# A two-layer encoder trunk in split float32: priority of one pair's sums, a scheduling edge for pair 0's accumulating transfers, and earlier low parts for the first mixer's output weights

## The chip, the cores and the metric

One NeuronCore of a Trainium2 chip runs the whole program. The metric is the device time of one execution in microseconds; of several runs the median counts. The engines are named as in the profile: PE is TensorE, DVE is VectorE, ACT is ScalarE, POOL is GpSimd, and SP is SyncE, which here only issues transfers.

## The reference

Two request groups, 512 and 256 tokens of 1024 numbers, go through the same trunk with the same weights. Nothing mixes the groups, so the kernel lays them side by side as 768 columns.

```
def even_layer(x, ...):
    x = x + 0.5 * swiglu(rmsnorm(x, f1_n), f1_g, f1_u, f1_d)
    x = x + mixer_ab(rmsnorm(x, mix_n), w_in, ..., w_out)
    x = x + 0.5 * swiglu(rmsnorm(x, f2_n), f2_g, f2_u, f2_d)
    return x

def odd_layer(x, ...):      # the same with mixer_c in the middle
    ...

def mixer_ab(h, w_in, ..., sink, w_out):
    z = h @ w_in
    a_out = u * vmix        # chunked spatial gating, u and v out of gelu(z[:, :1024])
    b_out = window_gqa(rope_partial(q), rope_partial(k), v, sink)
    return concatenate([a_out, b_out], axis=-1) @ w_out
```

The hidden width of the SwiGLU is 2816. A final rmsnorm follows the two layers.

## The kernel before

**Split float32.** Every product is made of three matmul passes on two-part numbers. A float32 tile is split into a high part, which is a rounded copy (`whi`, `oh`, `th`), and a low part, the difference (`wlo`, `ol`, `tl`). `wsplit` (L112) does it for weights: ACT makes the high part at L122, and DVE or POOL, by its argument `eng`, the low part at L123. POOL is the default. `split` (L206) does it for activations, always with ACT at L208 and DVE at L209. `mm3` (L188) then issues three matmuls of up to 512 columns at L152: high weight by high operand, high weight by low operand, low weight by high operand.

**The blocks.** Four half SwiGLU blocks (`ffn`) and two mixers alternate. In a block the gate and up weights are worked through in 11 pairs of 128-column tiles, by a scheme with seven products for a two-by-two blocking. It needs sums of weight tiles (`sums`, named `s1` to `s4`, L737). In the first four pairs (`EARLY`) the two products that need only the first half of the tokens come first, over all four pairs in the sequence `ORDERS`; each product's result is copied from PSUM by ACT into a tile `p1` (L602), and those copies are noted in the list `copied`. The first sum `s1` of these pairs isn't made by DVE but by the transfers: `added` loads one weight tile into a tile `s` and then a second one on top of it with an accumulating transfer. Both are issued by POOL at L107. For pair 0 this is called once, in the loop at the end of `ffn`, behind the ninth step of the sequence.

**The first mixer's end.** `mixer0` computes spatial gating and windowed attention; eight tiles `o` of 128 rows collect their outputs. `mixer_out` (L970) multiplies them by the output weights and adds the result to the residual, which was kept in DRAM (`xdm`) and comes back into tiles `xold`. Column tiles are called m = 0 to 7. `rows(m)` prepares the weights of one column tile: for even m it loads a 512 KB tile and a 256 KB tile `raw` by SP and splits the small one (for this and the next m, low part on DVE), then it splits its own half of the large one (low part on POOL). The tiles m = 0 and 1 (`alone`) are prepared ahead and begun while the attention of the last blocks still runs: k-tiles 4 and 5 first, then 0 to 3, first for the first 384 columns, then for the rest. After that the loop over m = 2 to 5 prepares and multiplies one column tile after the other. The attention chain is interleaved with it: scores on PE, mask and maximum on DVE (L1099), exponentials on ACT (L1105), scaling on DVE (L1115), transposes on PE (L156), `th` and `tl`, values on PE, and their sum into `o` on DVE (L1250).

**What sets the order.** PE's order is that of the code, with the interleaved chains placed by a counter of estimated PE time. On the other engines a list scheduler picks at compile time among ready instructions, by their place in the code and by `high_priority`; each engine then runs its list strictly in that order. `issue_after(ins)` queues those instructions of its block that run on the engine of `ins` behind `ins` in that list. It is no wait at run time. Tiles come from rotating pools: four `raw` buffers, five `whi` and five `wlo`. A transfer into a reused buffer waits until the last reader is done, and behind it waits all that SP has still to issue.

Of the kernel before, what the change touches and what calls it, by code (L numbers as in the profile page):

```python
# [16 lines left out]
P = 128  # L17
# [27 lines left out]
EARLY = 4  # L45
# [10 lines left out]
class Trunk:  # L56
# [421 lines left out]
    def ffn(self, pre):  # L478
# [2 lines left out]
            self.fw = self.open("work", self.other(self.guards["comb"][1]))  # L481
        rt, scales = self.acc, self.scales
        mixed = bool(self.unfed)
        urgent = 0 if self.first else EARLY - 1
        hs = {}

        etile = self.etile
# [36 lines left out]
        entries, entered, addeds = {}, {}, {}  # L524

        def pair(p):
# [12 lines left out]
            h = hs[p] = {}  # L539
# [3 lines left out]
            def sums(n, name):  # L543
                return self.sums(a[n, 1, 1], a[n, 1, 2], a[n, 2, 1], a[n, 2, 2], s, n, name)

            def parts(n, b):
                name = {"t2": "s2", "t3": "s3", "t1": "s1", "b22": "s4"}.get(b)
                with self.tc.high_priority() if b == "t2" and p == urgent else nullcontext():
                    return self.wsplit(sums(n, name) if name else a[n, 2, 2], nc.vector)

            def product(n, w, b, key, start, st=None):
# [95 lines left out]
            def entry():  # L647
                load((0, 1))
                return parts("gate", "t2")

            def settle(st):

                todo = [(n, b) for b in ("t2", "t3", "n4", "t1", "b22") for n in names]
                key = {"t1": "Z", "b22": "Z"}
                for i, (n, b) in enumerate(todo):
                    now, st = st, None
                    if i + 1 < len(todo):
                        st = parts(*todo[i + 1])
                    elif p + 1 < EARLY and (p % 2 or not p):
                        entered[p + 1] = entries[p + 1]()  # L660
                    if b == "t2":
                        begin(n, e[n, "p1"])
                    product(n, None, b, key.get(b, "Y"), b == "t1", now)
                    if b in ("t2", "t3"):
                        keep(b.replace("t", "u"), "Y", n)
                    elif b == "n4":
                        next(steps, None)
                    else:
                        add("Z", n, "u3" if b == "t1" else "u2")
                    if n == "up":  # L670
                        if b == "n4":
                            hidden(1, 0, bank["Y", "gate"], bank["Y", "up"])
                        elif b == "t1":
                            hidden(1, 1, e["gate", "u3"], e["up", "u3"])
                        elif b == "b22":
                            hidden(0, 1, e["gate", "u2"], e["up", "u2"])
# [30 lines left out]
        for i, p in enumerate(ORDERS[mixed]):  # L707
            next(stages[p])
            if i == 8:
                addeds[0]()  # L710
        for p in range(NPAIR):
            for _ in stages[p]:
                pass
# [256 lines left out]
    def mixer_out(self, name, ot, chain, cols=False, begun=None):  # L970

        nc = self.nc
        early, late = (4, 5, 0, 1, 2, 3) if cols else range(KD - 2), (KD - 2, KD - 1)
        oh, ol = ([self.gp.tile([P, T], F32R, tag=f"x{n}{k}", name=f"o{n}{k}") for k in range(KD)] for n in "hl")
        src = (oh, ol)
        self.x = [None] * KD
        old = {}

        def parts(ks, h):
            c0, c1 = HALVES[h]
            for k in ks:
                self.split(oh[k][:, c0:c1], ol[k][:, c0:c1], ot[k][:, c0:c1])

        def ready(ks, done=()):
            for h in (0, 1):
                parts([k for k in ks if (k, h) not in done], h)
            for k in ks:
                self.x[k] = self.xp.tile([P, T], F32, tag=f"x{k}", name=f"x{k}")  # L990
                if not cols:
                    nc.sync.dma_start(self.x[k], self.xd[k])

        def put(m, h, ps):

            c0, c1 = HALVES[h]
            x = self.x[m]
            if not cols:
                nc.vector.tensor_tensor(out=x[:, c0:c1], in0=ps[:, :H], in1=x[:, c0:c1], op=ALU.add)
                return  # L1000
            if h == 0:
                old[m] = self.rawp.tile([P, T], F32, tag="raw", name="xold")
                nc.sync.dma_start(old[m], self.xd[m])
            for a, b in ((H, TA), (TA, T)) if h else ((0, H),):
                out, rows = self.by_column(x, slice(0, P), a, b)
                nc.vector.tensor_tensor(out=out, in0=rows(ps[:, a - c0 : b - c0]), in1=rows(old[m][:, a:b]), op=ALU.add)

        def plus(m, h, ps):
            x = self.x[m][:, HALVES[h][0] : HALVES[h][1]]
            nc.vector.tensor_tensor(out=x, in0=ps[:, :H], in1=x, op=ALU.add)  # L1010
            self.final(m, *HALVES[h])

        loaded = {}

        def rows(m):
            if m % 2 == 0:
                loaded[4] = self.raw(name, 0, 4, m * P, 2 * P)
                loaded[2] = self.unit(name, 4, 2, m * P, 2 * P)
            c = m % 2 * P
            hi, lo = self.wsplit(loaded[4][:, :, c : c + P])  # L1020
            return [(hi[:, k, :], lo[:, k, :]) for k in range(4)] + [tuple(t[:, c : c + P] for t in k) for k in loaded[2]]

        def first(m, h, w):
            put(m, h, self.proj(w, src, HALVES[h], ks=early))

        def second(m, h):
            st = [tuple(t[:, k, m % 2 * P : m % 2 * P + P] for t in ends[m // 2]) for k in (0, 1)]
            plus(m, h, self.proj([None] * 6 + st, src, HALVES[h], ks=late))

        def end(i):  # L1030
            if i % 2 == 0:
                loaded["end"] = self.raw(name, KD - 2, 2, i * 2 * P, 4 * P)
            c = i % 2 * 2 * P
            ends.append(self.wsplit(loaded["end"][:, :, c : c + 2 * P]))

        alone = ()
        if begun:
            alone = (0, 1)
            w = [rows(m) for m in alone]
            done = [self.proj(w[m], begun, (0, H), ks=early[:2], last=False) for m in alone]  # L1040
            rest = early[2:]
            with self.tc.high_priority(), self.tc.issue_after(self.exps[-1]):
                parts(rest, 0)
            for m in alone:
                ps = self.proj(w[m], src, HALVES[0], ps=done[m], ks=rest, first=False)
                if m == 0:
                    parts(early, 1)
                    parts(early[:2], 0)
                    ready(early, [(k, h) for k in early for h in (0, 1)])
                put(m, 0, ps)  # L1050
            for m in alone:
                first(m, 1, w[m])
        else:
            ready(early)
        for m in range(len(alone), KD - 2):
            w = rows(m)
            for h in (0, 1):
                first(m, h, w)
        self.drain(chain)
        with self.tc.issue_after(self.exps[-1]):  # L1060
            self.silu()
        ready(late)
        self.ffn_open(self.close("mp"))
        self.ffn_tiles()
        self.mixed = True
        self.norm_begin(self.following)
        ends = []
        w = rows(6)
        end(0)
        first(6, 0, w)  # L1070
        end(1)
        for m in (0, 1):
            second(m, 0)
        first(6, 1, w)
        for m in (2, 3):
            second(m, 0)
        w = rows(7)
        end(2)
        for h in (0, 1):
            first(7, h, w)  # L1080
        end(3)
        for m in range(4, KD):
            second(m, 0)
        self.half_done(0)
        for m in range(KD):
            second(m, 1)
        self.close("xg")
        self.fw = self.open("work", self.other(self.guards["comb"][1]))
        self.half_done(1)
# [732 lines left out]
```

## Time and profile before

| | us |
|---|---|
| three runs, median (lowest to highest) | 2595.53 (2593.48 to 2601.28) |
| the profiled execution | 2594.83 |
| its span | 2593.1 |
| PE busy | 2552.5 |
| DVE busy | 2231.6 |
| ACT busy | 1366.2 |
| POOL busy | 159.3 |

The span runs from the first to the last instruction; the execution's own time is 1.7 us longer. PE's granted clock was 0.997 of full speed over the span. Rows of the timeline give start, duration, engine, line, operation and tiles; in brackets stands the idle time ahead of the row and what ended it. An instruction's duration overlaps the next one's start a little, so the distance from start to start is what one costs in a full queue.

### The profile page before, as it was taken

How to read it: one execution, taken by the hardware profiler on the slowest of the kernel's cores; microseconds unless marked ns; L12 is line 12 of the kernel's file. 1: busy time of each engine (PE TensorE's matmuls, PEld its weight loads, DVE VectorE, ACT ScalarE, POOL GpSimd, SP SyncE). 2: the span in 40 equal slices, each digit the busy share in tenths (PEclk: the TensorE clock that was granted, in tenths of full speed). 3: DMA queues.
4: the chain of work that ended last, by engine and by line, in shares of the span. 5: the costliest groups of instructions: out<-in, count | busy, mean ns of one | idle time of the engine just before them, and what ended most of it. 6: DMA issues, size and time to landing. Idle time of an engine off the chain costs nothing.

```text
span 2593.1 us, 41320 instructions
## 1 busy us (share of the span) xinstructions
PE 2552.5 (98%) x15114; PEld 2487.0 (96%) x15114; DVE 2231.6 (86%) x4659; ACT 1366.2 (53%) x2869; POOL 159.3 (6%) x255
## 2 busy tenths in 40 slices
PE   9999999999999999999999999999999999999998
PEld 8999999988899999999999999998998999999997
DVE  7988898889789989889998889986767699888897
ACT  7544454556656545445654445454545465444543
POOL 1000000000121000000100000001222220000000
PEclk9999999999999999999999999999999999999999
DMA  7523222421144322222532222242221343222212
GB/s 256 160 85 102 72 80 68 134 90 52 50 128 130 114 66 74 74 72 92 142 103 82 66 82 66 66 145 64 64 64 41 106 134 119 82 72 76 72 65 75
DMA packets 93372, 238.68 MB, mean 92 GB/s; under 512 B 21488, under 2 KB 34288, under 8 KB 93168
## 3 DMA queue, kind: packets, MB, share of 16 engines
q1 hardware_dynamic: 85712, 218.96, 26.4%
q0 software_dynamic: 7168, 16.78, 3.0%
q8 instruction: 119, 1.95, 0.3%
q14 instruction: 85, 0.70, 0.1%
q10 hardware_dynamic: 288, 0.29, 0.0%
HBM read 226.56 MB, written 15.07 MB: 93 GB/s over the span
## 4 chain that ended last, share of the span: by engine, by line
PE 67%; DVE 4%; ACT 1%; issue 1%; DMA 0%; DVEq 0%; ACTq 0%
PE ps_mm L152 41%; PE ps_aux L152 25%; PE ps_aux L156 1%; DMA raw<-in_w 0%; DVE wlo L123 0%; DVE tmp L415 0%; ACT p L1105 0%; DVE p L1115 0%; DVE p L1099 0%; ACT whi L122 0%; DVE s L737 0%; DVE tl L209 0%; DVE qk L1579 0%; DVE sg L589 0%; DVE t21l L209 0%
## 5 line engine op out<-in xcount | busy, mean ns | idle before, releaser
L122 ACT CAST whi<-s 128x512 fp32r<-128x512 f32 x496 | 304.7, 620 | 408.2 <-DVE s L737 184.3
L122 ACT CAST whi<-raw 128x512 fp32r<-128x512 f32 x504 | 305.9, 619 | 226.6 <-PE ps_mm L152 93.5
L123 DVE TENSOR_TENSOR wlo<-s,whi 128x512 fp32r<-128x512 f32 x496 | 336.7, 684 | 60.2 <-ACT whi L122 52.6
L123 DVE TENSOR_TENSOR wlo<-raw,whi 128x512 fp32r<-128x512 f32 x468 | 320.1, 692 | 18.6 <-ACT whi L122 15.0
L152 PE MATMUL ps_aux<-dt,whi 128*128 128x384 f32 x864 | 219.2, 334 | 0.0
L152 PE MATMUL ps_mm<-db,whi 128*128 128x384 f32 x864 | 219.2, 334 | 0.0
L152 PEld LDWEIGHTS ps_aux<-dt,whi 128*128 128x128 f32 x864 | 156.0, 188 | 0.0
L152 PEld LDWEIGHTS ps_mm<-db,whi 128*128 128x128 f32 x864 | 156.0, 188 | 0.0
L152 PE MATMUL ps_aux<-dt,wlo 128*128 128x384 f32 x432 | 144.4, 334 | 1.4 <-DVE wlo L123 1.4
L152 PE MATMUL ps_mm<-xh,whi 128*128 128x512 f32 (+1 forms) x416 | 145.6, 350 | 0.0
L152 PE MATMUL ps_mm<-db,wlo 128*128 128x384 f32 x432 | 144.3, 334 | 0.0
L152 PE MATMUL ps_mm<-xh,wlo 128*128 128x512 f32 (+1 forms) x416 | 140.9, 339 | 0.0
L152 PE MATMUL ps_mm<-xl,whi 128*128 128x512 f32 (+1 forms) x416 | 140.9, 339 | 0.0
L737 DVE TENSOR_TENSOR s<-raw,raw 128x512 f32<-128x512 f32 x124 | 84.0, 685 | 26.6 <-DMA raw<-in_w 26.3
L577 DVE TENSOR_TENSOR u<-ps_aux,u 128x384 f32<-128x384 f32 x176 | 96.9, 551 | 4.6 <-PE ps_aux L152 4.3
L152 PE MATMUL ps_aux<-dh,whi 128*128 128x384 f32 x384 | 97.5, 334 | 0.0
L793 DVE TENSOR_TENSOR x<-ps_aux,x 128x384 f32<-128x384 f32 x160 | 85.2, 550 | 14.1 <-PE ps_aux L152 13.9
L1105 ACT ACTIVATE p<-p,st 128x256 f32<-128x256 f32 (+3 forms) x144 | 68.9, 480 | 50.2 <-DVE st L1103 50.1
L123 POOL TENSOR_TENSOR wlo<-raw,whi 128x512 fp32r<-128x512 f32 x36 | 48.5, 1355 | 720.8 <-ACT whi L122 707.3
L572 ACT COPY u<-ps_mm 128x384 f32<-128x384 f32 x176 | 83.5, 474 | 17.0 <-PE ps_mm L152 16.6
L793 DVE TENSOR_TENSOR x<-ps_mm,x 128x384 f32<-128x384 f32 x160 | 86.0, 550 | 6.9 <-PE ps_mm L152 6.6
L107 POOL DMA_DIRECT2D s<-in_w x64 | 47.0, 762 | 700.6 <-PE ps_aux L152 387.0
(516 smaller groups left out, 8172.7 us busy)
## 6 DMA issues: line engine op xcount, KB each, us to landing
raw<-in_w SPq DMA_DIRECT2D x346, 512.0 KB, 3.7
s<-in_w POOLq DMA_DIRECT2D x64, 256.0 KB, 5.0
xdm<-x SPq DMA_DIRECT2D x16, 384.0 KB, 2.4
x<-in_x SPq DMA_DIRECT2D x16, 192.0 KB, 5.9
tok<-in_xt SPq DMA_DIRECT2D x12, 256.0 KB, 6.7
xold<-xdm SPq DMA_DIRECT2D x8, 384.0 KB, 3.1
x<-xdm SPq DMA_DIRECT2D x8, 384.0 KB, 4.7
out_y<-y SPq DMA_DIRECT2D x8, 384.0 KB, 2.4
```

Source lines behind the costliest of these rows:

```text
L107: (eng or self.nc.sync).dma_start(raw, src, **kw)
L122: nc.scalar.copy(hi, src)
L123: (eng or nc.gpsimd).tensor_tensor(out=lo, in0=src, in1=hi.bitcast(F32), op=ALU.subtract)
L152: self.nc.tensor.matmul(out, lhsT=lhsT, rhs=rhs, start=start, stop=stop, **kw)
L156: self.nc.tensor.transpose(out, src, self.ident)
L572: nc.scalar.copy(e[n, out], bank[key, n])
L577: nc.vector.tensor_tensor(out=t, in0=bank[key, n], in1=t, op=ALU.add)
L737: f = lambda o, x, y, op: self.nc.vector.tensor_tensor(out=o, in0=x, in1=y, op=op)
L793: nc.vector.tensor_tensor(out=o, in0=ps, in1=o, op=ALU.add)
L1105: ins = nc.scalar.activation(outs[i], outs[i], AF.Exp, bias=nm[:, i : i + 1], accum_out=sm[:, i : i + 1])
```

## The change

Three edits are made.

1. In the first block the first sums (for the product `t2`) of pair 3 are traced at high priority as well as those of pair 0; in the other blocks it stays with pair 3 alone.
2. In every block the call of pair 0's `added` stands in an `issue_after` of a copy of `p1`: the fourth copy of the block in the first block (pair 1's second), the sixth elsewhere.
3. In the first mixer's `mixer_out`, `rows(2)` is called earlier, right after the first product of m = 0, and the low parts of m = 0, 1 and 2 are made by DVE. Those of m = 3 and later stay on POOL; the second mixer passes no `begun` and keeps all on POOL.

```diff
-        urgent = 0 if self.first else EARLY - 1
+        urgent = (0, EARLY - 1) if self.first else (EARLY - 1,)
+        behind = len(self.copied) + (3 if self.first else 5)
...
-                with self.tc.high_priority() if b == "t2" and p == urgent else nullcontext():
+                with self.tc.high_priority() if b == "t2" and p in urgent else nullcontext():
...
             if i == 8:
-                addeds[0]()
+                with self.tc.issue_after(self.copied[behind]):
+                    addeds[0]()
...
-            hi, lo = self.wsplit(loaded[4][:, :, c : c + P])
+            hi, lo = self.wsplit(loaded[4][:, :, c : c + P], self.nc.vector if begun and m < 3 else None)
...
                 if m == 0:
+                    w.append(rows(len(alone)))
                     parts(early, 1)
...
         else:
+            w = []
             ready(early)
         for m in range(len(alone), KD - 2):
-            w = rows(m)
+            st = w.pop() if m < len(w) else rows(m)
             for h in (0, 1):
-                first(m, h, w)
+                first(m, h, st)
```

With `alone` of two tiles, `w` holds m = 0, 1 and 2 when the loop begins, so m = 2 is taken from it and from m = 3 on `rows` is called as before.

In the instruction lists of the five engines nothing differs between the two programs outside the first mixer's output stage, neither in the sequence nor in which engine waits for which: the copies that edit 2 names run on ACT, the transfers in its block on POOL. In the output stage PE's sequence is the same as well. SP issues the two `raw` loads of m = 2 ahead of the first two `xold` loads, where they stood behind them. POOL has three low parts fewer. DVE's list shows where they went; the numbers belong to tiles and let a tile be followed.

First place on DVE: the attention step of the last-but-one prompt block, whose scaled sums go to `o2`, and the low parts `tl` of the next step's probabilities. Before:

```order
L1356 TENSOR_TENSOR o2_5932<-o2_5932,ug_7395 128x512
L1250 TENSOR_TENSOR o6_5936<-ps_aux505_7403,tb_7408 64x2x64 x2
L1250 TENSOR_TENSOR o7_5937<-ps_aux505_7403,tb_7408 64x2x64 x2
L1356 TENSOR_TENSOR o2_5932<-o2_5932,ug_7435 128x256
L209 TENSOR_TENSOR tl_7468<-ps_aux509_7462,th_7467 128x512
```

And now:

```order
L1254 TENSOR_TENSOR o7_5937<-ps_aux505_7403,tb_7408 64x2x64 x2
L1360 TENSOR_TENSOR o2_5932<-o2_5932,ug_7435 128x256
L123 TENSOR_TENSOR wlo519_7614<-raw112_7605,whi519_7613 128x512
L123 TENSOR_TENSOR wlo520_7618<-raw112_7605,whi520_7617 128x512
L209 TENSOR_TENSOR tl_7468<-ps_aux509_7462,th_7467 128x512
```

The low parts of m = 0 and 1 have moved from POOL to the place right ahead of the three `tl`.

Second place on DVE, one attention step later: behind the last `o3` come three `tl`, then the score rows (ISA) of the next step, then the low parts `ol` of the output operand. Before:

```order
L1356 TENSOR_TENSOR o3_5933<-o3_5933,ug_7581 128x256
L209 TENSOR_TENSOR tl_7658<-ps_aux523_7652,th_7657 128x512
L209 TENSOR_TENSOR tl_7667<-ps_aux524_7661,th_7666 128x512
L209 TENSOR_TENSOR tl_7676<-ps_aux525_7670,th_7675 128x512
L209 TENSOR_TENSOR ol4_7601<-o4_5934,oh4_7593 128x384
L1099 ISA p_7696,st_7700<-ps_aux526_7682,msk_5700,sink_5702 128x256
```

And now:

```order
L1360 TENSOR_TENSOR o3_5933<-o3_5933,ug_7581 128x256
L123 TENSOR_TENSOR wlo528_7723<-raw115_7720,whi528_7722 128x512
L209 TENSOR_TENSOR tl_7658<-ps_aux523_7652,th_7657 128x512
L209 TENSOR_TENSOR tl_7667<-ps_aux524_7661,th_7666 128x512
L209 TENSOR_TENSOR tl_7676<-ps_aux525_7670,th_7675 128x512
L123 TENSOR_TENSOR wlo529_7727<-raw114_7718,whi529_7726 128x512
L1103 ISA p_7696,st_7700<-ps_aux526_7682,msk_5700,sink_5702 128x256
```

Both low parts of m = 2 are made here now, one ahead of the `tl` and one in the place of `ol4`, which follows behind the eight score rows; the five `ol` that stood behind the score rows follow it in the same sequence.

Third place on DVE, where m = 0 and 1 are added to the residual (`x0`, `x1`) and the shared low part of m = 2 and 3 (`wlo531`) stood. Before:

```order
L1250 TENSOR_TENSOR o7_5937<-ps_aux529_7774,tb_7781 64x2x64 x2
L1006 TENSOR_TENSOR x0_7736<-ps_mm528_7758,xold_7740 128x4x64
L123 TENSOR_TENSOR wlo531_7818<-raw115_7815,whi531_7817 128x512
L1006 TENSOR_TENSOR x1_7737<-ps_mm530_7792,xold_7755 128x2x64
L1006 TENSOR_TENSOR x1_7737<-ps_mm530_7792,xold_7755 128x4x64
```

And now:

```order
L1254 TENSOR_TENSOR o7_5937<-ps_aux531_7786,tb_7793 64x2x64 x2
L1008 TENSOR_TENSOR x0_7748<-ps_mm530_7770,xold_7752 128x4x64
L1008 TENSOR_TENSOR x1_7749<-ps_mm532_7804,xold_7767 128x2x64
L1008 TENSOR_TENSOR x1_7749<-ps_mm532_7804,xold_7767 128x4x64
L209 TENSOR_TENSOR tl_7838<-ps_aux534_7832,th_7837 128x512
```

The low part that stood between `x0` and `x1` is gone from here; it is `wlo528` of the second place.

## The prediction

> **What bounds the kernel now.** I read the page first, for the engine that carries the span, then PE's waits in the stretch of the first mixer's end, then the rows there.
>
> ```profile
> span 2593.1 us, 41320 instructions
> ...
> PE 2552.5 (98%) x15114; PEld 2487.0 (96%) x15114; DVE 2231.6 (86%) x4659; ACT 1366.2 (53%) x2869; POOL 159.3 (6%) x255
> ```
>
> PE is busy for 2552.5 of 2593.1 us. No edit adds or removes a matmul, so all that can move is PE's idle time, 40.6 us over the whole program, and of that only what lies where instructions move. Edits 1 and 2 leave every engine's list and waits as they were. So only edit 3 counts, and it acts from about 668 us on. The waits of PE from 655 to 780 us (waiting line, released by, us in total, times, longest):
>
> ```profile
> PE ps_mm L152 <- DVE wlo L123: 1.8, 1, 1.8
> PE ps_aux L152 <- DVE tl L209: 1.1, 2, 0.9
> PE ps_mm L152 <- DVE ol L209: 0.8, 1, 0.8
> ```
>
> Three entries, 3.7 us, all ended by DVE. PE's rows show the last and the first of them:
>
> ```profile
> 689.79 0.33 PE L152 MATMUL ps_mm<-ol,whi 128*128 128x384 f32 x1
> ...
> 691.27 0.34 PE L152 MATMUL ps_mm<-oh,whi 128*128 128x384 f32 x1
> 692.44 0.44 PE L152 MATMUL ps_mm<-ol,whi 128*128 128x384 f32 x1 [0.84 <-DVE ol L209]
> ...
> 698.48 0.33 PE L152 MATMUL ps_mm<-oh,whi 128*128 128x384 f32 x1
> 698.65 0.34 PE L152 MATMUL ps_mm<-ol,whi 128*128 128x384 f32 x1
> 700.81 0.45 PE L152 MATMUL ps_mm<-oh,wlo 128*128 128x384 f32 x1 [1.81 <-DVE wlo L123]
> ```
>
> A matmul of 384 columns follows its predecessor by 0.17 us here (698.48 and 698.65). So the first stall costs 1.17 - 0.17 = 1.00 us and the second 2.16 - 0.17 = 1.99 us. **2.99 us is the most that this stage can give directly.**
>
> **The second stall.** PE waits there for the shared low part of m = 2. The DVE rows:
>
> ```profile
> 684.81 0.42 DVE L1356 TENSOR_TENSOR o<-o,ug 128x256 f32<-128x256 f32 x1
> 685.78 1.89 DVE L209 TENSOR_TENSOR tl<-ps_aux,th 128x512 fp32r<-128x512 f32 x3 [0.55 <-ACT th L208]
> 687.59 0.55 DVE L209 TENSOR_TENSOR ol<-o,oh 128x384 fp32r<-128x384 f32 x1
> ...
> 689.67 0.55 DVE L209 TENSOR_TENSOR ol<-o,oh 128x384 fp32r<-128x384 f32 x1
> 690.14 0.17 DVE L1103 TENSOR_SCALAR st<-st 128x4 f32<-128x4 f32 x1
> 690.21 0.55 DVE L209 TENSOR_TENSOR ol<-o,oh 128x384 fp32r<-128x384 f32 x1
> 690.68 1.24 DVE L1109 TENSOR_TENSOR st<-sink,st 128x4 f32<-128x4 f32 x1
> 691.84 2.42 DVE L209 TENSOR_TENSOR ol<-o,oh 128x384 fp32r<-128x384 f32 x5
> ...
> 699.62 0.61 DVE L1006 TENSOR_TENSOR x<-ps_mm,xold 128x256 f32<-128x256 f32 x1
> 700.08 0.68 DVE L123 TENSOR_TENSOR wlo<-raw,whi 128x512 fp32r<-128x512 f32 x1
> 700.67 0.86 DVE L1006 TENSOR_TENSOR x<-ps_mm,xold 128x128 f32<-128x128 f32 x2
> ```
>
> The low part runs at 700.08 only because of its place in the list, behind the residual sum of m = 0. In the changed list it stands ahead of the three `tl` of 685.78, some 15 us before PE needs it. Its inputs must be there by then:
>
> ```profile
> 662.42 9.29 SPq L107 DMA_DIRECT2D raw<-in_w  x2
> ...
> 700.26 0.88 SPq L1003 DMA_DIRECT2D xold<-xdm  x2
> 701.23 0.86 SPq L107 DMA_DIRECT2D raw<-in_w  x2
> ```
>
> Today the two loads of m = 2 are issued from 662.42 on; they move ahead of two `xold` loads and so become earlier still, while those `xold` loads take the places of 662.42 and later, and m = 0's is first read behind the five `ol`, at 694 us. So the low part is ready and **1.99 us go**.
>
> **The first stall.** PE waits for `ol` of k-tile 1, which sat behind a sum on four numbers that took 1.24 us (690.68). A POOL low part ran at that time:
>
> ```profile
> 668.27 3.08 POOL L123 TENSOR_TENSOR wlo<-raw,whi 128x512 fp32r<-128x512 f32 x2 [559.31 <-ACT whi L122]
> 690.32 1.59 POOL L123 TENSOR_TENSOR wlo<-raw,whi 128x512 fp32r<-128x512 f32 x1 [18.96 <-ACT whi L122]
> 696.27 1.43 POOL L123 TENSOR_TENSOR wlo<-raw,whi 128x512 fp32r<-128x512 f32 x1 [4.37 <-ACT whi L122]
> ```
>
> The same sum takes 0.16 us when POOL is idle:
>
> ```profile
> 676.01 0.16 DVE L1109 TENSOR_TENSOR st<-sink,st 128x4 f32<-128x4 f32 x1
> ```
>
> So POOL's instruction of 690.32 cost DVE 1.08 us. It moves to DVE, where a low part costs 0.60 us from start to start (700.08 to 700.67). I add up DVE's new list from the end of the `o` row at 685.18. The first low part fills the idle 0.55 us and ends at 685.78; three `tl`, 1.81, to 687.59; the second low part, 0.60, to 688.19; the score rows, as long as before (688.05 to 689.67, 1.62), to 689.81; then `ol` of k-tile 4 at 0.47 to 690.28, `st` 0.10, `ol` of 5 to 690.85, the sum on four numbers, now 0.10, `ol` of 0 to 691.42, `ol` of 1 to 691.89, visible to PE some 0.1 us later. PE asks for the first of these at 689.79 and now waits some 0.6 us there, then keeps step and reaches the matmul of 692.44 at about 692.05. The old stall of 1.00 becomes one of 0.61: **0.39 us go**.
>
> [...]
>
> **What is added ahead of the scores.** The low parts of m = 0 and 1 now stand ahead of the `tl` at 671.74:
>
> ```profile
> 670.53 1.10 DVE L1356 TENSOR_TENSOR o<-o,ug 128x256 f32<-128x256 f32 x1
> 671.74 1.89 DVE L209 TENSOR_TENSOR tl<-ps_aux,th 128x512 fp32r<-128x512 f32 x3
> ```
>
> They cost 2 x 0.60 = 1.20 us. The `o` row took 1.10 us beside POOL and 0.42 without it (684.81); it gives back 0.68, so it ends at 670.87, the low parts at 672.07, and the `tl` start 0.33 us late. PE's next scores reuse the PSUM banks that `tl` frees:
>
> ```profile
> 659.10 0.43 PE L152 MATMUL ps_aux<-kh,q 64*128 64x384 f32 x1 [0.90 <-DVE tl L209]
> ...
> 672.59 0.45 PE L152 MATMUL ps_aux<-kh,q 64*128 64x384 f32 x2
> ...
> 684.47 1.47 PE L156 MATMUL ps_aux<-ident,p 128*128 128x128 f32 x12
> ```
>
> At 672.59 PE doesn't wait, two steps earlier it did. What margin it has isn't shown; the cost lies between 0 and 0.33 us, or 1.20 if POOL's block weren't given back. I take 0.2. Behind the `tl` the score rows and exponentials slide by the same third of a microsecond; the transposes that need them come at 684.47, so nothing is late.
>
> **The sum.** 1.99 + 0.39 - 0.2 = 2.2 us less. The profiled execution took 2594.83, of which the span is 2593.1: that gives 2592.6. The median shown, 2595.53, is 0.7 above the profiled one and gives 2593.3. **I say 2593.0.** A measurement tells a difference of some 0.3%, 7.8 us, from none; this is a tenth of a per cent.
>
> **Does the gain last?** From 700.81 to 780 us PE works without a pause, so whatever feeds it must come 2.2 us sooner. The tightest place:
>
> ```profile
> 708.71 1.15 ACT L122 CAST whi<-raw 128x512 fp32r<-128x512 f32 x2 [5.32 <-DMA raw<-in_w]
> ...
> 712.38 2.18 DVE L1115 TENSOR_SCALAR p<-p,st 128x256 f32<-128x256 f32 x4
> ...
> 715.49 1.03 PE L156 MATMUL ps_aux<-ident,p 128*128 128x128 f32 x8
> ```
>
> ACT is held until 708.71 by the load of m = 4, the exponentials queue behind it, and the scaled `p` end at 714.56, 0.9 us before PE transposes them. If that load came no sooner, PE would stall there for up to 714.56 - (715.49 - 2.2) = 1.3 us. But today the load is issued behind two `xold` loads of 384 KB at 700.26, with which it shares the DMA engines; in the changed list those two find free buffers earlier (the ones of m = 2's loads) and are out of the way. I expect the load some 3 us sooner, as these rows have it: 768 KB in 3 to 4 us of which the two others need no more.
>
> ```profile
> raw<-in_w SPq DMA_DIRECT2D x346, 512.0 KB, 3.7
> ...
> xold<-xdm SPq DMA_DIRECT2D x8, 384.0 KB, 3.1
> ```
>
> **The rivals.**
> - The gain is caught at 715.49, as worked out: 2.2 - 1.3 = 0.9 us less, 2593.9. For it speaks the long wait of ACT for that load, against it the freer DMA queue.
> [...]
> - Slower: SP's queue decides. The `xold` load of m = 3 now takes the buffer whose last reader is the POOL low part of 696.27 (m = 3), and the loads of m = 4 stand behind it. If that reader slips, ACT's high parts of 708.71 slip with it, and the `p` behind them. By one batch of exponentials, the 2.5 us between the rows of 709.86 (708.71 and 1.15) and 712.38, the `p` would end at 717.1 and PE's transposes of 715.49 come 1.6 us late: 2596.4. It decides from 0.9 us of delay on. Against it: that low part ends at 697.70, 2.6 us ahead of today's issue, and its place in the lists is the same.
> - The lists don't tell all, and the first block's transfers or sums do move. PE's idle time there is the stake:
>
> ```profile
> sum 60.00, PE 53.59 PEld 49.72 DVE 46.14 ACT 47.16 POOL 7.77; mean PE 17.86 PEld 16.57 DVE 15.38 ACT 15.72 POOL 2.59
> ```
>
> In the first 60 us PE is idle for 6.4. At most that goes on top: 2592.6 - 6.4 = 2586.2. Against it: the named copies are ACT's and the transfers POOL's, and no wait differs.
>
> **How the numbers follow.** The forecast has 0.66, the caught gain 0.15, no change 0.09, slower 0.06, the first block 0.04. The range: the forecast with nothing lost is 2594.83 - 2.99 = 2591.8, and the lowest run stands 1.4 below the profiled execution, so 2590.4; above, the slower rival, 2596.4, on the profiled basis, and 0.3 of the 0.7 by which the median stands above it, 2596.7. Faster by over 0.3% would need under 2587, which only the extreme of the first block's case reaches, 0.02. Slower by over 0.3% has no mechanism but runs like the highest one, 2601.28, 0.02. The rest is the same, 0.96.
>
> **What would show it.** Right: no wait of PE for `wlo` near 700; one of about 0.6 us on `ol` near 690; three POOL low parts fewer; the sum on four numbers near 690 back at 0.16 us; the load of m = 4 landed by 706; the first 660 us alike to a few tenths. Wrong: a wait on `tl` near 672 of over 0.5 us, a wait of PE on `p` or `ident` near 713, or a first block whose waits have changed.

## The result and the profile after

| | before | after |
|---|---|---|
| median, us | 2595.11 (22 runs, lowest 2590.67) | 2591.17 (22 runs, lowest 2588.33) |
| span of the profiled execution, us | 2593.1 | 2588.6 |
| PE idle within the span, us | 40.6 | 36.4 |

The ratio is 0.9986, with a 95% interval of 0.998 to 0.9992: 3.6 us less, between 2.1 and 5.2. By the bound of 0.3% this is no change; it is still a gain that the runs can tell from zero. The forecast was 2593.0, 2.2 us less, with a range of 2590.4 to 2596.7. One run of each kernel was disturbed (8802 and 2783 us) and is left out of the ratio.

The page of the changed kernel, span and engines:

```profile
span 2588.6 us, 41317 instructions
...
PE 2552.2 (99%) x15114; PEld 2487.2 (96%) x15114; DVE 2232.6 (86%) x4662; ACT 1366.6 (53%) x2869; POOL 155.5 (6%) x252
```

PE does the same 15114 matmuls in nearly the same time (0.3 us less). Three low parts went from POOL to DVE, as the counts show (252 after 255, 4662 after 4659). Of the 4.5 us between the two spans 4.2 are idle time of PE. PE's waits from 655 to 780 us (in total, times, longest):

```profile
PE ps_aux L152 <- DVE tl L209: 1.2, 3, 0.9
PE ps_mm L152 <- DVE ol L209: 0.4, 1, 0.4
```

The wait for `wlo` of 1.8 us is gone, that for `ol` is half as long. PE's rows at the two places, the second where the stall of 700.81 was (everything lies 1.7 us later in this trace, by chance, as more profiles show below):

```profile
691.70 0.34 PE L152 MATMUL ps_mm<-oh,whi 128*128 128x384 f32 x1
692.48 0.44 PE L152 MATMUL ps_mm<-ol,whi 128*128 128x384 f32 x1 [0.45 <-DVE ol L209]
...
700.26 0.33 PE L152 MATMUL ps_mm<-ol,whi 128*128 128x384 f32 x1
700.44 0.33 PE L152 MATMUL ps_mm<-oh,wlo 128*128 128x384 f32 x1
```

From 691.70 to 692.48 it is 0.78 us; less the usual step of 0.17, the first stall cost 0.61. The `oh,wlo` pass at 700.44 follows its predecessor by 0.18: no stall is left. DVE's rows show why:

```profile
672.59 1.28 DVE L123 TENSOR_TENSOR wlo<-raw,whi 128x512 fp32r<-128x512 f32 x2
673.79 1.88 DVE L209 TENSOR_TENSOR tl<-ps_aux,th 128x512 fp32r<-128x512 f32 x3
...
687.26 0.69 DVE L123 TENSOR_TENSOR wlo<-raw,whi 128x512 fp32r<-128x512 f32 x1
687.86 1.88 DVE L209 TENSOR_TENSOR tl<-ps_aux,th 128x512 fp32r<-128x512 f32 x3
689.66 0.68 DVE L123 TENSOR_TENSOR wlo<-raw,whi 128x512 fp32r<-128x512 f32 x1
...
692.88 0.15 DVE L1113 TENSOR_TENSOR st<-sink,st 128x4 f32<-128x4 f32 x1
```

The shared low part of m = 2 stands ahead of the three `tl` in the list, so it is the row of 687.26. It now ends at 687.95, twelve microseconds ahead of PE's pass of 700.44; the other low part of m = 2 ends at 690.34. The sum on four numbers takes 0.15 us, not 1.24, because POOL starts its first low part only afterwards. POOL, ACT and SP of the same trace:

```profile
697.89 1.40 POOL L123 TENSOR_TENSOR wlo<-raw,whi 128x512 fp32r<-128x512 f32 x1 [586.56 <-DVE p L1119]
...
706.73 1.14 ACT L122 CAST whi<-raw 128x512 fp32r<-128x512 f32 x2 [3.83 <-DMA raw<-in_w]
...
664.14 35.50 SPq L1005 DMA_DIRECT2D xold<-xdm  x4
701.95 2.20 SPq L107 DMA_DIRECT2D raw<-in_w  x2
```

The four `xold` loads stand ahead of m = 4's weights now, and these land 4.8 us after their issue (701.95 to 706.73). Before it was 7.5 (701.23 to 708.71).

**Matmul against matmul.** Both traces hold the same 15114 matmuls in one sequence, so I subtract the start of each in one trace from its start in the other and read where the difference changes. That needs no judgement on which idle time counts. After minus before, in us, at places given in the time of before:

```
 60      570     668     680     691     697     703     715     775
+2.06   +1.36   +1.73   +2.05   +2.75   +1.61   -0.51   -0.52   -0.49
```

From 668 to 715 us the changed kernel gains 2.25 us: it loses 0.32 at 672 and 0.70 at 690, and gains 1.14 at 692 and 2.12 at 700. It starts 2 us late, and between 2090 and 2110 us it gains 3.0 more. Whether those two belong to the change, the experiments tell.

### The profile page after: what moved, and what is told of

Same layout as the page of the kernel before. It is cut to its first block, busy times and chain, and to the rows that moved or that the text cites. A ratio compares the mean times of both kernels' runs of the same rounds, so it can differ in the third digit from the quotient of the medians.

```text
span 2588.6 us, 41317 instructions
## 1 busy us (share of the span) xinstructions
PE 2552.2 (99%) x15114; PEld 2487.2 (96%) x15114; DVE 2232.6 (86%) x4662; ACT 1366.6 (53%) x2869; POOL 155.5 (6%) x252
## 4 chain that ended last, share of the span: by engine, by line
PE 89%; DVE 6%; ACT 2%; DMA 1%; issue 1%; SPq 0%; DVEq 0%; ACTq 0%
PE ps_mm L152 54%; PE ps_aux L152 34%; PE ps_aux L156 1%; DVE wlo L123 1%; ACT p L1109 1%; DVE p L1103 1%; DMA raw<-in_w 1%; DVE tl L209 0%; DMA x<-in_x 0%; DVE tmp L415 0%; DVE p L1119 0%; ACT whi L122 0%; DVE s L739 0%; DMA first<-in_w 0%; DVE o L1254 0%
## 5 line engine op out<-in xcount | busy, mean ns | idle before, releaser
L152 PEld LDWEIGHTS ps_mm<-xh,whi 128*128 128x128 f32 x416 | 79.8, 192 | 9.3 <-issue 0.9
```

Source lines behind the costliest of these rows:

```text
L152: self.nc.tensor.matmul(out, lhsT=lhsT, rhs=rhs, start=start, stop=stop, **kw)
```

## The experiments

The ratio is always to the kernel before, measured in alternation on the same chip. The code cuts leave lines out, also where no dots stand. "Local" is the change of the matmuls' offset against the profile of before between 668 and 715 us, as in the table above.

### Edits 1 and 2 alone

```
-        urgent = 0 if self.first else EARLY - 1
+        urgent = (0, EARLY - 1) if self.first else (EARLY - 1,)
+        behind = len(self.copied) + (3 if self.first else 5)
...
-                addeds[0]()
+                with self.tc.issue_after(self.copied[behind]):
+                    addeds[0]()
```

> Edits 1 and 2 alone, without edit 3; every engine's list and waits are those of before. Theory A (edits 1 and 2 do nothing): ratio to before 1.000 within 0.001, PE's stalls near 692 and 701 us of 0.8 and 1.8 us as before. Theory B (they give the 1.4 us by which the result lies beyond the 2.2 of the forecast): 1 to 2 us faster than before, and a first 60 us in which PE is idle for less than 6.4 us. The trace also gives a second profile of the program of before: if the wait of 2.9 us near 2106 us is chance (A), it is likely to have another length here; if it belongs to the program of before (theory C), it is 2.5 to 3 us again.

Measured: 2594.04 us, ratio 0.9998 (0.9989 to 1.0007), against 2593.92 of before. Both stalls are there:

```profile
692.19 0.44 PE L152 MATMUL ps_mm<-ol,whi 128*128 128x384 f32 x1 [0.83 <-DVE ol L209]
700.63 0.60 PE L152 MATMUL ps_mm<-oh,wlo 128*128 128x384 f32 x1 [1.93 <-DVE wlo L123]
```

So these two edits are worth nothing that can be measured. The offsets also lose 0.26 us at 672, though no low part was moved. Something else stands out in this trace: the matmul of 700.63 takes 0.60 us where 0.44 or 0.45 stood in other traces, and the matmuls behind the stall fall 1.6 us further back, more than the stall itself explains. The busy time by stretch shows what it is (us, PE busy and instructions, PEld, DVE, ACT, POOL, then the granted clock, DMA share, GB/s):

```profile
700.80:704.20 3.40, 3.40 (x14) 3.30 (x15) 0.99 (x3) 0.80 (x2) 0.00 (x0) 0.50 0.84 276
704.20:707.60 3.40, 3.40 (x27) 3.02 (x26) 2.46 (x9) 0.76 (x2) 0.00 (x0) 1.00 0.52 192
```

The granted clock is 0.50 for one stretch of 3.41 us right behind the stall: 14 matmuls instead of 27. The first profile of before has no such stretch here. I took this up as **theory E**: the stall of 1.9 us sometimes also halves the clock behind it.

### Edit 3 alone

```
+            hi, lo = self.wsplit(loaded[4][:, :, c : c + P], self.nc.vector if begun and m < 3 else None)
...
+                    w.append(rows(len(alone)))
...
+            st = w.pop() if m < len(w) else rows(m)
```

> Edit 3 alone; the lists are those of the changed kernel. Theory A: ratio as the changed kernel's, 0.9986 within its interval (about 3 us faster), and PE's time between the matmuls of about 632 and 760 us 2.2 to 2.5 us shorter than before. Theory B: only 1.5 to 2.5 us faster than before. Theory C: no wait near 2102 us again; A: it may be there or not.

Measured: 2589.44 us, ratio 0.9988 (0.9979 to 0.9997), local -2.23. There is no stall near 700, and this at the first:

```profile
690.04 0.44 PE L152 MATMUL ps_mm<-ol,whi 128*128 128x384 f32 x1 [0.45 <-DVE ol L209]
```

Edit 3 alone gives what all three give together.

### The early call with the low parts on POOL

The changed kernel, with `rows(2)` called early but every low part of the large weight tiles left on POOL (the shared one is DVE's in all versions):

```
-            hi, lo = self.wsplit(loaded[4][:, :, c : c + P], self.nc.vector if begun and m < 3 else None)
+            hi, lo = self.wsplit(loaded[4][:, :, c : c + P])
```

> The changed kernel, with the early call of rows(2) kept but all low parts of the large weight tiles on POOL again. Theory A (the place of the shared low part is what counts): PE's stall on the weights near 701 us stays gone (1.99 us less), the POOL low part of m = 2 now blocks DVE some 6 us sooner, so the stall on ol near 692 is 0.4 to 1.2 us; between 632 and 760 us 1.8 to 2.4 us shorter than before. Rival D (the engine is what counts, since POOL blocks DVE): under 1 us shorter than before.

Measured: 2591.45 us, ratio 0.9989 (0.998 to 0.9997), local -2.21. PE and POOL:

```profile
687.11 0.38 PE L152 MATMUL ps_aux<-kh,q 64*128 64x256 f32 x1 [0.61 <-DVE tl L209]
...
683.82 1.28 POOL L123 TENSOR_TENSOR wlo<-raw,whi 128x512 fp32r<-128x512 f32 x1 [12.88 <-ACT whi L122]
```

POOL's low part of m = 2 runs six microseconds sooner (683.82, before 690.32). What it blocks now is DVE's `ol` of 684.01:

```profile
684.01 1.50 DVE L209 TENSOR_TENSOR ol<-o,oh 128x384 fp32r<-128x384 f32 x1
...
691.26 0.15 DVE L1113 TENSOR_TENSOR st<-sink,st 128x4 f32<-128x4 f32 x1
```

That `ol` takes 1.50 instead of 0.55 us, and the `tl` behind it come late, so PE waits 0.61 us there; the sum near 691 is free, and PE doesn't wait for `ol` any more. The expected stall on `ol` of 0.4 to 1.2 us did not come; it turned into this one on `tl`. The balance is the same: PE loses nothing at 672 and 1.0 us at 687, and gains 1.09 at 692 and 2.11 at 700. So the early call gives the gain, and with it the engine on which the low parts run makes no difference here.

### The low parts on DVE, without the early call

Before, with only the `wsplit` line of edit 3.

> The kernel of before with the low parts of m = 0, 1 and 2 on DVE, but rows(2) at its old place. The small sum near 690 us is back at 0.16 us, so the stall on ol (1.00 us) goes. Theory A: the shared low part stays behind the residual sums, and PE still waits 0.8 to 2 us for weights near 700 us; between 632 and 760 us 0.8 to 1.9 us shorter than before. Rival D: 2.0 us shorter or more, as the changed kernel.

Measured: 2593.57 us, ratio 1.0000 (0.9991 to 1.0008). The first stall is gone, the second is not:

```profile
704.63 0.45 PE L152 MATMUL ps_mm<-oh,wlo 128*128 128x384 f32 x1 [1.92 <-DVE wlo L123]
```

The offsets lose 0.33 us at 672 and gain 1.11 at 692: 0.8 us, less than the interval can tell. A stretch at half clock follows the stall here too. It costs 1.0 us up to 703 us and another 0.6 up to 715, so this profile ends the stretch 0.83 us behind the one of before, where 0.8 to 1.9 us less were expected.

### The shared low part early, m = 2's own part late

By the rows, the changed kernel's remaining stall on `ol` comes from the two low parts ahead of the score rows. So I called only the load early, and `rows(2)` behind the parts of the output operand:

```
                 if m == 0:
-                    w.append(rows(len(alone)))
+                    load(len(alone))
                     parts(early, 1)
                     parts(early[:2], 0)
+                    w.append(rows(len(alone)))
                     ready(early, [(k, h) for k in early for h in (0, 1)])
```

> The changed kernel, with the loads and the shared low part of m = 2 early as there, but its own low part split off and made behind the five ol. Theory A: both stalls shrink: the one on ol near 690 us to 0 to 0.3 us (DVE's list ahead of the ol is 0.6 us shorter), none near 700; between 632 and 760 us 2.4 to 3.0 us shorter than before (the changed kernel 2.1), and no half-clock stretch there. Rival: the own part now comes late for PE and takes the place of the stall that went, 0.5 to 1.5 us near 700.

Measured: 2590.10 us, ratio 0.9984 (0.9976 to 0.9993), local -2.23 as with the changed kernel. This is a miss, as 2.4 to 3.0 were expected. No low part runs ahead of the `tl` any more, but the scheduler put one into the gap behind them, and the other comes late, at 693.76. DVE and PE:

```profile
687.64 0.68 DVE L123 TENSOR_TENSOR wlo<-raw,whi 128x512 fp32r<-128x512 f32 x1
689.86 0.55 DVE L209 TENSOR_TENSOR ol<-o,oh 128x384 fp32r<-128x384 f32 x1
...
690.47 0.44 PE L152 MATMUL ps_mm<-ol,whi 128*128 128x384 f32 x1 [0.45 <-DVE ol L209]
```

One low part still stands between the `tl` and the `ol`, and the stall is 0.45 us as before.

### Four more profiles of before, and one more of the changed kernel

> The kernel of before, unchanged, for another profile. Theory E: the stall of 1.8 to 1.9 us near 701 us costs more than its own length, since in some executions a stretch of 3.41 us at half clock follows it (1.7 us more); of the three profiles with that stall so far two have the stretch and one hasn't. E expects the stall of 1.8 to 1.9 us again, and the stretch right behind it in about two of three. Against E: no such stretch in any further profile with the stall. The wait of 2.9 us near 2106 us of the first profile is expected not to be there (chance), under 1.5 us instead.

> As before_second_profile: the stall near 701 us of 1.8 to 1.9 us; by theory E a half-clock stretch of 3.41 us behind it in about two of three profiles.

> The kernel before once more, for its profile alone. Theory E (the stall of about 1.9 us at 700 us sometimes also halves the granted clock for 3.41 us, which costs about 1.7 us more): the stall is there again, 1.8 to 1.95 us, and in about 3 of 5 profiles with the stall a stretch at clock 0.5 lies within 10 us behind it, against 0 of 5 without the stall. E is weakened if both this and the fifth profile lack it.

> The kernel before, one more profile of it, read as the fourth is: the stall near 700 us of 1.8 to 1.95 us is there; by theory E a stretch of 3.41 us at clock 0.5 lies behind it in about 3 of 5 profiles; without E it would lie there no oftener than in the kernels that lack the stall, 0 of 5.

> The changed kernel again. No stall near 700 us, and by theory E no stretch at clock 0.5 between 690 and 760 us. Ratio to the kernel before 0.998 to 0.9992. The start of the program, which was 2 us later in the first profile of this kernel than in that of before, should lie within the spread of the other profiles (idle 6.4 to 8.3 us in the first 60 us) if that was chance.

Each took one time as well: 2591.86, 2590.61, 2593.62 and 2593.81 us for before. The changed kernel gave 2589.79, ratio 0.9987 (0.9978 to 0.9997), local -2.21.

*The start and 2106 us.* At 60 us the five profiles of before (the first one is zero) lie between -0.48 and +1.24, and the changed kernel, at +2.06 in its first profile, at -0.27 in its second. The late start was chance. Between 2090 and 2110 us the four new profiles of before gain 1.1 to 3.0 us against the first one, which had a wait of 2.88 us there; the changed kernel gains 3.0 in its first profile and loses 0.8 in its second. Neither belongs to the change.

*The clock.* All four have the stall near 700, of 1.81 to 1.92 us, and two of them a stretch at half clock right behind it. The fourth, ahead of the stretch and in it, and the fifth, with its stall and behind it:

```profile
697.00:701.40 4.40, 2.59 (x16) 2.24 (x15) 3.91 (x10) 0.00 (x0) 0.19 (x1) 1.00 0.16 39
701.40:704.80 3.40, 3.40 (x15) 2.96 (x15) 1.38 (x2) 1.17 (x2) 0.00 (x0) 0.50 0.89 333
```

```profile
700.00:703.40 3.40, 1.48 (x9) 1.16 (x7) 3.33 (x10) 0.00 (x0) 0.04 (x1) 1.00 0.00 0
703.40:706.80 3.40, 3.40 (x26) 3.11 (x28) 2.00 (x4) 1.07 (x2) 0.00 (x0) 1.00 0.78 272
```

The same stall, and afterwards 15 matmuls in the one and 26 in the other. Over all profiles: with the stall 4 of 7 have the stretch within 2 us behind it (before 2 of 5, edits 1 and 2, the late low parts); without it none of 7 has one between 690 and 760 us, the changed kernel's second profile among them:

```profile
697.00:700.40 3.40, 3.40 (x24) 3.37 (x24) 3.33 (x10) 0.99 (x2) 0.00 (x0) 1.00 0.39 120
700.40:703.80 3.40, 3.40 (x27) 3.02 (x26) 2.97 (x11) 0.09 (x1) 0.00 (x0) 1.00 0.75 231
```

The stretch costs 1.5 to 1.7 us: up to 715 us those traces of the same lists are 1.57 and 1.51 us behind the first profile of before, the two without it -0.03 and +0.11 us.

The timed executions say the same without a trace. Each gives its mean granted clock. Of the first four experiments, which ran on one chip, the two with the stall had 0.9958 (22 executions) and the two without it 0.9963 (22), a difference of 0.00045 with a standard error of 0.00025. With the executions of before on that chip, and the kernels of two more chips compared each on its own, there are 99 executions with the stall and 45 without (the kernels with the wait of the next section left aside): the difference is 0.00038, with a standard error of 0.00015. One stretch lowers the mean by 0.5 x 3.41 / 2590 = 0.00066, so this is 0.6 of a stretch in each execution, near the 4 of 7.

### A true wait in the first block

`issue_after` set an order but no wait. Here the first block's accumulating transfers do wait for the fourth copy of `p1`: POOL first reads one column of it.

```
-                with self.tc.issue_after(self.copied[behind]):
+                after = self.copied[behind]
+                if begins:
+                    after = nc.gpsimd.tensor_scalar(
+                        out=self.ngains[:, 56:57], in0=self.p1s[behind][:, 0:1], scalar1=-1.0, scalar2=None, op0=ALU.mult
+                    ).ins
+                with self.tc.issue_after(after):
                     addeds[0]()
```

> The changed kernel, in which the first block's POOL transfers do wait at run time: POOL first computes on one column of the fourth copy p1, and the transfers stand behind that instruction. So what edit 2 names is done by this. Theory A: the transfers of pair 0 start at about 27 us instead of 5 and 11 and take no bandwidth from the first loads; PE's idle time in the first 60 us falls by 0 to 2 us, or rises by up to 3 where the sums of pair 0 (due at 40 us) then wait; within 0.1% of the changed kernel. Rival F (the wait is worth having): 2 us or more less idle in the first 60 us, ratio to before 0.9978 or lower.

> The changed kernel with a real wait of the first block's accumulating transfers for the fourth copy of p1, timed beside the changed kernel on one chip. Theory A (that wait is worth nothing that can be told): the two differ by less than their intervals tell. Rival F (it is worth 2 us at the start): at least 2 us below the changed kernel, and PE idle under 6.4 us in the first 60 us, as the first time (6.27).

Measured: 2588.70 us, ratio 0.9983 (0.9974 to 0.9991), and beside the changed kernel 2589.02, ratio 0.9982 (0.9974 to 0.9991), where the changed kernel had 2589.79 and 0.9987 (0.9978 to 0.9997). POOL issues those transfers from 25 us on, where the first profile of the changed kernel has them from 5.7. The first 60 us of the second profile of this kernel, and then of the changed one:

```profile
0.00:60.00 60.00, 54.24 (x270) 50.10 (x271) 47.28 (x118) 47.88 (x109) 8.35 (x18) 1.00 0.83 257
```

```profile
0.00:60.00 60.00, 53.10 (x266) 49.29 (x267) 46.42 (x116) 47.46 (x109) 8.18 (x17) 1.00 0.79 254
```

PE is idle for 5.76 us here and 6.27 in the first profile of it; the twelve others have 6.41 to 8.25. So the wait probably gains about 1 us at the start, as the medians' 0.8 would have it. It isn't the 2 us that the rival asked for, and the intervals don't part it from the changed kernel. This is the fastest version that was run, by its medians.

## Why the prediction was right, and what it left out

**What bounds the kernel, and that only edit 3 counts.** Shown: edits 1 and 2 alone have a ratio of 0.9998, edit 3 alone 0.9988. The first block's rival (they do move) fell with that. One sign that the forecast named did not hold: the first 660 us were to be alike to a few tenths, and the changed kernel was 2.06 us late at 60 us. Single profiles of the kernel before differ there by 1.7 us, so this sign could not tell the rivals apart.

**The second stall, 1.99 us.** Shown: 2.12 in the offsets, and the stall returns as soon as the early call is taken away (1.92 us with the late low parts). Its mechanism was the forecast's: the place in DVE's list.

**The first stall, 1.00 to 0.61 us.** Measured 0.61, by 0.70 lost at 690 and 1.14 won at 692, which leaves 0.44 gained where 0.39 was forecast. The cause, the sum that POOL blocked, shows in its 0.15 us, and again in the experiment with POOL: its low part came six microseconds sooner and the stall on `ol` was gone, without any work moved to DVE. There the block fell on other work and cost PE 1.0 us at 687.

**The low parts ahead of `tl`, 0.2 us.** The term was a little small: PE lost 0.32 at 672, the upper bound of 0.33 from the rows, and nothing where the low parts stayed on POOL. PE had next to no margin there. The 0.26 of edits 1 and 2 alone show that a loss of this size can also come without the moved parts. Together with the first stall this leaves 0.1 us, so nearly all of the stage's gain is the second stall's.

**The sum.** Forecast -2.2; -2.19 to -2.25 in the five profiles with the changed lists in this stage.

**That the gain lasts.** Shown: from 703 to 775 us the offset stays within 0.03 us, PE doesn't wait at the transposes, and m = 4's weights come 4.8 us after their issue instead of 7.5. In the time of before they were there at 705.0 (706.73 less 1.73), where 706 was the condition. The rival in which the gain is caught there, and the slower one through SP's queue, both needed a late load.

**No change (0.09).** That outcome did not come: the ratio's interval, 0.998 to 0.9992, leaves 1 out. With the early call the engine of the low parts made no difference: local -2.21 with them on POOL and -2.23 with them on DVE. At the old place the move won 0.8 us of PE's time in the trace; its ratio, 1.0000 (0.9991 to 1.0008), can't tell that from nothing. What paid was the place. In the forecast's first-stall term I had counted the engine's change as the cause of the gain; it was one of two ways to get the same.

**What the forecast lacked.** The runs gave -3.6, the stage -2.2, and the interval of 2.1 to 5.2 alone doesn't part the two. All runs together do: in each of the four sets of runs the kernels with the early call (without the true wait) were by their means 3.6 to 3.9 us faster than those with the lists of before, together 3.7 with a standard error of 0.35. So the direction and the places were right by the mechanism, but the size was about 1.5 us short. One part that was missing goes with the clock: half clock followed the stall of 1.9 us in 4 of 7 profiles, at 1.6 us each, and in none of the 7 without the stall. That is 0.9 us on average, and 2.2 + 0.9 = 3.1. The term that was mis-sized is the second stall's: by this it should have been about 2.9 and not 1.99. The first profile of before was one in which the clock stayed up, so its rows could not show it. Where the remaining 0.6 us come from stays open; they are less than two standard errors. The late start and the wait at 2106 us, which make the two first profiles differ by more than this, were chance.

## What to carry to other kernels

When PE waits for an instruction that was ready long before, look for its place in the list: calling it earlier gave 2.2 us of PE's time here on either engine, while moving other work to another engine at the old place gave 0.8 us in the trace and nothing that the runs could tell. Price a stall of PE by its idle time plus the chance of a slow stretch behind it (here 1.8 to 1.9 us, and 1.6 more in 4 of 7 profiles), and take that chance from several profiles. Before a difference between two profiles is put down to a change, take the kernel before once or twice more: two of the three largest differences between the first two profiles were not the change's.

## What the hardware showed

**Half clock after a short stall.** Apart from the one at the program's end, the first profile of before has two stretches at granted clock 0.5, of 6.83 us from 149.4 on and of 3.41 from 582.9; the first of the changed kernel has four of 3.41 us, from 27.0, 153.3, 583.4 and 634.6. These are stalls of PE in the profiles, by length, with the time at which they end and whether half clock lies within 2 us behind it (in the row of 150.72 it begins 1.3 us ahead of the end):

```
stall, us   ends at    profile                half clock
1.43         630.90    before                 no
1.44         632.63    changed                yes
1.45         291.20    before                 no
1.45         292.56    changed                no
1.8      near 700       before, fourth         yes
1.81         700.81    before                 no
1.81         700.18    before, third          no
1.82         699.94    before, second         yes
1.9      near 703       before, fifth          no
1.92         704.63    late low parts         yes
1.93         700.63    edits 1 and 2          yes
2.07        2101.20    changed, second        yes
2.88        2106.51    before                 no
3.35          26.86    changed                yes
3.47         150.72    before                 yes
3.47         152.81    changed                yes
```

The length of a stall doesn't settle it: 1.81 and 2.88 us were not followed by half clock where 1.82 and 2.07 were. Nor is a long stall needed: near 582 us half clock begins with a longest stall of 0.63 us ahead of it (579.81 in before, 0.62 at 581.16 in the changed kernel), beside matmuls on 64 of 128 rows, and the mean clock from 575 to 600 us is 0.93 in each of the first six profiles. What decides was not shown, and no stall was placed on purpose. The stall of 2.07 us at 2101 us stands in a kernel without the one at 700; the clock in 3.4 us with it and in the next 3.4:

```profile
2097.80:2101.20 3.40, 1.33 (x8) 1.04 (x7) 3.40 (x6) 2.23 (x6) 1.32 (x1) 1.00 0.00 0
2101.20:2104.60 3.40, 3.40 (x11) 3.40 (x12) 3.40 (x6) 3.31 (x7) 2.38 (x3) 0.50 0.15 57
```

**POOL and DVE.** A sum on four numbers a row took 1.24 us on DVE beside a POOL low part (690.68 in before) and 0.15 without one (692.88 in the changed kernel). An `ol` took 1.50 us beside one (684.01, the low parts on POOL) and 0.55 without (687.59 in before).
